# Where the residual rows, a quarter of a weight and the last splits of a one-core hybrid layer are placed

## The chip, the cores and the metric

The kernel runs on one core of a Trainium2 chip. A core has five engines that run side by side, each in its own order: TensorE (PE in the profile; its weight loads are PEld), VectorE (DVE), ScalarE (ACT), GpSimd (POOL) and SyncE (SP), which here issues most DMAs. Sixteen DMA engines move data between the device memory and the on-chip memory. Matmuls write to PSUM, everything else that is kept on the chip lies in SBUF.

The metric is the device time of one execution in microseconds (us), as the median of several. Inputs are laid out by the host before the launch, so that every weight load is one contiguous transfer of 1 MB.

## The reference

One decoder layer on 256 positions of width 2048. The parts that matter here are at its end: the state-space branch with its GLU, the merge of three branches, the output projection, the norm and the residual.

```python
h = rms_norm(x, pre_g)
proj = h @ w_in
a_u, a_v, a_g, b_x, b_g, x_q, x_g, gate_logits = jnp.split(proj, splits, axis=-1)
y_a = spatial_gating(a_u, a_v, sg_ln_g, sg_ln_b, sg_w, sg_b) * jax.nn.silu(a_g)
y_b = s5_branch(b_x, a_re, a_im, log_dt, b_re, b_im, c_re, c_im, d, glu_w, glu_b) * jax.nn.silu(b_g)
y_x = memory_cross_attention(x_q, rms_norm(mem, mem_g), xa_wk, xa_wv) * jax.nn.silu(x_g)
ys = jnp.stack([y_a, y_b, y_x], axis=2)
branch = jnp.einsum('bsnc,ncd->bsnd', ys, w_branch)
gates = jax.nn.sigmoid(gate_logits.reshape(bsz, seq, N_BRANCH, D_MODEL))
merged = jnp.sum(gates * branch, axis=2)
out = merged @ w_out
return x + rms_norm(out, post_g)
```

Inside `s5_branch` the last step is `y * sigmoid(y @ glu_w + glu_b)`. All is float32.

## The kernel before

**Arithmetic.** Each float32 operand of a product is split into a high part (`a.copy` on ACT, a cast to the type fp32r) and a low part (a subtraction on DVE), by `split_to`. A product is three matmuls: high by high, high by low, low by high. A weight of 1 MB is loaded by `load` into one of three `raw` buffers of 128 x 2048, and split in halves of 128 x 1024 into one of four `hl` buffers by `split`. So a `raw` buffer is free again when the subtractions of both its halves have run, and a cast into an `hl` buffer waits until PE has used the half that was four before it.

**Order.** PE's order is the program's. The order on the other engines, SP's DMAs among them, is fixed when the kernel is built: a planner takes, of what it thinks ready, the instruction of the earliest rank. The rank is the place in the program; `tc.high_priority(offset=AHEAD)`, which `split` uses, sets it 250 places ahead. Buffers of a pool are handed out in the planner's order as well. On the chip every engine then runs its own list strictly in order, so an instruction that waits holds up all behind it. `tc.keep_in_program_order` keeps marked instructions in the program's order.

**Stages at the end, with the start of each in the trace.** The gate product of the state-space branch runs up to 749 us. Then come:

- The GLU stage (749 to 770 us): four loads of `glu`; `ahead(0, ...)` splits half of the fourth quarter of the output weight into homes of its own (`room(8)`, `room(12)`: eight 128 x 512 tiles of the pool of h's splits, no longer needed), and `spread` loads the rows of `g_post` into `room(0)` and those of `x[0]` into `room(4)`, four DMAs of 256 KB each.
- The branch stage (770 to 812 us): for four column blocks c, two loads of `w_br`, products, gating and merging. `merge_t(c)`, run in the background by `pump`, transposes the merged block and makes the operands of the later products: the splits `mm`, and for a Strassen-like scheme on the first half of the depth and width of the output product the forms `S3` (from `r3`, kept with `r21` in the tile with tag `cb`) and, for c of 2 and 3, `S1`, `S2`, `S4`. The subtractions of `S1` and `S4` run on POOL.
- The output stage (from 812 us): `normal(0)`, `normal(1)`, `normal(2)`, product X, then the rows of `x[1]` by `spread` into four tiles of tag `s`, `normal(3)`, product Y, `narrow(0)`, product X by `S2` and a stored sum of weights (`wsum[1]`), `ahead(1, ...)` with the fourth quarter's other half into a tile of tag `cb` and one of tag `H2` (where `S2` was), `narrow(1)`, product Z by `S1` and `wsum[0]`, product Y by `S4` and the fourth quarter (`b22`), product Z by `S3` and `wsum[2]`, product X by `wsum[3]`.
- The last product (from 884.73 us): 256 columns, first the one half of the rows (tb 0), then the other. Its first half-load is split into `room(8)` and `room(12)`, its other three into `hl` buffers.
- The finish: squares, root, gain and residual, and the stores. `part` finds the tile and columns of `g_post` or `x` that a piece needs.

The matmuls of a weight half take 2.6 us in `normal` and 1.3 us in `product`; a 1 MB load takes some 4.8 us from issue to landing.

Of the kernel before, what the change touches and what calls it, by code (L numbers as in the profile page):

```python
# [9 lines left out]
F32 = mybir.dt.float32  # L10
F32R = mybir.dt.float32r
# [3 lines left out]
ALU = mybir.AluOpType  # L15
# [3 lines left out]
P = 128  # L19
D = 2048  # L20
# [13 lines left out]
AHEAD = 250  # L34
# [9 lines left out]
def trunk(ctx: ExitStack, tc: tile.TileContext, I, out):  # L44
    nc = tc.nc
    v, a, g, pe = nc.vector, nc.scalar, nc.gpsimd, nc.tensor
# [8 lines left out]
    s5p = ctx.enter_context(tc.tile_pool(name="s5p", bufs=2))  # L55
    s5c = ctx.enter_context(tc.tile_pool(name="s5c", bufs=1))
# [8 lines left out]
    def nm(s):  # L65
        n_[0] += 1
        return f"{s}_{n_[0]}"

    def slot(tag, shape, dt=F32):
        return big.tile(shape, dt, tag=tag, name=nm(tag))  # L70
# [5 lines left out]
    def load(src):  # L76
        t = rawp.tile([P, 2048], F32, tag="raw", name=nm("raw"))
        nc.sync.dma_start(out=t, in_=src)
        return t
# [8 lines left out]
            split_to(hi, lo, src)  # L88
        return hi, lo

    def split_to(hi, lo, src, eng=None):
        a.copy(out=hi, in_=src)  # L92
        (eng or v).tensor_tensor(out=lo, in0=src, in1=hi.bitcast(F32), op=ALU.subtract)  # L93

    def rsqrt(src, n):
        y = small([P, n])
# [136 lines left out]
    def tm_quarter(acc, raw, hl, kq, nk):  # L233
        for hf in range(2):
            wh, wl = split(raw[:, hf * 1024:(hf + 1) * 1024])
            for k in range(2):
                kk = kq * 4 + hf * 2 + k
                sl = slice(k * 512, (k + 1) * 512)
                for tb in range(2):
                    tm_mm(acc[tb], wh[:, sl], wl[:, sl], hl[kk], tb, kk == 0, kk == nk - 1)  # L240
            pump(rate["tm"])
# [23 lines left out]
    for pc in range(8):  # L265
# [6 lines left out]
        wh, wl = (z.rearrange("p (q n) -> p q n", q=2) for z in halves(CM_OFF))  # L272
# [680 lines left out]
    def room(i0):  # L953
        return [xp.tile([P, 512], F32R, tag=f"x{i0 + k}", name=nm("xr")) for k in range(4)]

    def ahead(kq, homes):
        raw = load(I["w_out"][1, 2 + kq])
        for k in range(4):
            t, i = homes[k // 2], k % 2
            split_to(t[i], t[2 + i], raw[:, k * 512:(k + 1) * 512])  # L960
            b22.append((t[i], t[2 + i]))

    post = {}

    def spread(key, src, homes):
        post[key] = [t.bitcast(F32) for t in homes]
        for k in range(4):
            tc.keep_in_program_order(nc.sync.dma_start(out=post[key][k], in_=src[:, k * 512:(k + 1) * 512]))

    sgB = [slot("H1", [P, D]), slot("H2", [P, D])]  # L970
    for c in range(4):
# [11 lines left out]
    for bp in range(4):  # L983
        ps = acc_tile()
        raw = load(I["glu"][bp])
        for b in range(2):
            wh, wl = split(raw[:, b * 1024:(b + 1) * 1024], CM_OFF)
            cm_half(ps[:, b], wh, wl, ygl, 0, 8)
        t = fold(ps, None)
        for i in range(2):  # L990
            a.activation(out=t[:, i, :], in_=t[:, i, :], func=AF.Sigmoid, bias=glu_b[:, 2 * bp + i:2 * bp + i + 1])
        b = slice(2 * bp, 2 * bp + 2)
        v.tensor_tensor(out=t, in0=t, in1=u[:, b, :], op=ALU.mult)
        v.tensor_tensor(out=t, in0=t, in1=sb[:, b, :], op=ALU.mult)
        for i in range(2):
            d = yB[2 * bp + i]
            split_to(d[:, 0], d[:, 1], t[:, i])
        if bp == 0:
            ahead(0, [room(8), room(12)])
        elif bp == 1:  # L1000
            spread("g", I["g_post"][0].broadcast_to([P, D]), room(0))
        elif bp == 2:
            spread(0, I["x"][0], room(4))

    yBs = [Plain(d, True) for d in yB]
    mm = {}
# [9 lines left out]
    S1, S2, S4 = [], [], []  # L1016

    def merge_t(c):
        yield from steps(3 if c >= 2 else 2)
        for hf in range(2):  # L1020
            tp = (yp if hf else miscp).tile([P, 2, T], F32, tag="y" if hf else "misc", name=nm("mt"))
            for i in range(2):
                db = c * 4 + hf * 2 + i
                for tb in range(2):
                    pe.transpose(tp[:, i, tb * P:(tb + 1) * P], mg[tb][:, db * P:(db + 1) * P], ident)
            yield None
            d = mm_tile(c)[:, 2 * hf:2 * hf + 2]
            split_to(d[:, :, 0], d[:, :, 1], tp)
            k = slice((c % 2) * 4 + 2 * hf, (c % 2) * 4 + 2 * hf + 2)
            lo_, up = tp[:, :, 0:P], tp[:, :, P:T]  # L1030
            if c < 2:
                a.copy(out=r21[:, k], in_=up)
                v.tensor_tensor(out=r3[:, k], in0=lo_, in1=r21[:, k], op=ALU.subtract)
                split_to(S3[:, k, 0], S3[:, k, 1], r3[:, k])
            else:
                if not S1:
                    S1.append(slot("H1", [P, 8, 2, P], F32R))
                    S2.append(slot("H2", [P, 8, 2, P], F32R))
                    S4.extend(s5p.tile([P, 2, 2, P], F32R, tag=f"P{i // 2 + 1}", name=nm("S4")) for i in range(4))
                t = wk.tile([P, 3, 2, P], F32, tag="w0", name=nm("sa"), padded_shape=[P, 4, 2, P])  # L1040
                tt(t[:, 0], r21[:, k], up, ALU.subtract)
                stt(t[:, 1], r3[:, k], -1.0, up, ALU.mult, ALU.subtract)
                tt(t[:, 2], lo_, t[:, 1], ALU.add)
                split_to(S1[0][:, k, 0], S1[0][:, k, 1], t[:, 0], g)
                split_to(S2[0][:, k, 0], S2[0][:, k, 1], t[:, 1])
                f = S4[k.start // 2]
                split_to(f[:, :, 0], f[:, :, 1], t[:, 2], g)
            if hf == 0:
                yield None

    def product(ps, form, src):
        for kk in range(8):
            if src is b22:
                wh, wl = src[kk]
            else:
                if kk % 4 == 0:
                    raw = load(src[kk // 4])
                if kk % 2 == 0:
                    hi, lo = split(raw[:, kk % 4 * 512:kk % 4 * 512 + 1024])
                sl = slice(kk % 2 * 512, (kk % 2 + 1) * 512)  # L1060
                wh, wl = hi[:, sl], lo[:, sl]
            f = form[kk]
            pe.matmul(ps, lhsT=f(0), rhs=two(wh), start=kk == 0, stop=False)  # L1063
            pe.matmul(ps, lhsT=f(0), rhs=two(wl), start=False, stop=False)  # L1064
            pe.matmul(ps, lhsT=f(1), rhs=two(wh), start=False, stop=kk == 7)  # L1065
            if kk % 4 == 3:
                pump(0.0)

    for c in range(4):
        Bp = acc_tile()  # L1070
        for kq in range(2):
            tm_quarter([Bp[:, 0], Bp[:, 1]], load(I["w_br"][1, c, kq]), yBs, kq, 8)
        for tb in range(2):
            d = sgB[tb][:, csl(c)]
            v.tensor_tensor(out=d, in0=Bp[:, tb], in1=d, op=ALU.mult)
            v.tensor_tensor(out=mg[tb][:, csl(c)], in0=mg[tb][:, csl(c)], in1=d, op=ALU.add)
        bg[2].append(merge_t(c))
# [9 lines left out]
        a.activation(out=t, in_=ps, func=AF.Square, scale=D ** -0.5, accum_out=ssq[:, tb, n:n + 1])  # L1087

    def part(key, lo_, hi_):
        return post[key][lo_ // 512][:, lo_ % 512:(hi_ - 1) % 512 + 1]  # L1090

    def gated(dst, ps, lo_, hi_):
        v.tensor_tensor(out=dst, in0=ps, in1=part("g", lo_, hi_), op=ALU.mult)
# [8 lines left out]
    def cut(t):  # L1102
        return [t[:, i] for i in range(4)]
# [28 lines left out]
    normal(1)  # L1132
    normal(2)
    product(X, a11, w_o[0, 0:2])
    spread(1, I["x"][1], [s5p.tile([P, 512], F32R, tag="s", name=nm("xs"), bufs=4) for _ in range(4)])
    sn = snap_tile()
    s1, c11 = sn[:, 0], sn[:, 1]
    a.copy(out=s1, in_=X)
# [2 lines left out]
    sq_out(1, N[:, 1], 2, csl(2))  # L1141
    gated(og[0][:, csl(2)], N[:, 0], 1024, 1536)
    gated(N[:, 1], N[:, 1], 1024, 1536)
    product(Y, a12, w_o[0, 2:4])
    tt(c11, s1, Y, ALU.add)
    sq_out(0, c11, 0, csl(0))
# [3 lines left out]
    sn = snap_tile()  # L1150
    s2, s5 = sn[:, 0], sn[:, 1]
    tt(s2, X, s1, ALU.add)
    ahead(1, [cut(s5c.tile([P, 4, 512], F32R, tag="cb", name="bq")), cut(slot("H2", [P, 4, 512], F32R))])
    narrow(1)
    sq_out(0, c3[0][:, 0:T], 3, slice(1536, 1792))
    sq_out(1, c3[1][:, 0:T], 3, slice(1536, 1792))
# [33 lines left out]
    for kh in range(2):  # L1190
        raw = load(I["w_out3"][1, kh])
        for hf in range(2):
            src = raw[:, hf * 1024:(hf + 1) * 1024]
            if kh == 0 and hf == 0:
                for i, t in enumerate((room(8), room(12))):
                    wh, wl = t[0], t[1]
                    split_to(wh, wl, src[:, i * 512:(i + 1) * 512])
                    wks += [(wh[:, k * T:(k + 1) * T], wl[:, k * T:(k + 1) * T]) for k in range(2)]
            else:
                wh, wl = split(src)  # L1200
                wks += [(wh[:, k * T:(k + 1) * T], wl[:, k * T:(k + 1) * T]) for k in range(4)]
# [13 lines left out]
    for tb in range(2):  # L1215
# [4 lines left out]
        c = slice(tb, tb + 1)  # L1220
# [118 lines left out]
```

## Time and profile before

| | before |
|---|---|
| median of 3 runs | 911.99 us (911.44 to 912.46) |
| profiled execution, its own time | 911.15 us |
| its span in the profile | 909.3 us |
| PE busy | 894.4 us (98%) |
| DVE busy | 787.4 us (87%) |
| ACT busy | 591.3 us (65%) |
| POOL busy | 78.6 us (9%) |
| DMA, mean over the span | 240 GB/s |
| PE's last matmul starts | 901.30 us |

Busy time is the time in which an engine has an instruction running. For PE it says little: matmuls overlap, and a PE that is slowed or waits for a fraction of a step still counts as busy. More can be read from the starts of its matmuls: two that follow without a wait start 0.22 us apart at 512 columns and 0.11 us apart at 256. In the timelines below, the first column is the start in us from the start of the span, the second the duration (of all, where xN instructions are merged into one row), then engine, line, operation, what is written and read, shapes; in brackets stands how long the engine was idle before, and what ended that. In the rows of windows, each engine has its busy time and its count in the order PE, PEld, DVE, ACT, POOL; then follow the granted TensorE clock, the DMA engines' busy share and GB/s. In the rows of waits stand the total in us, the number of waits and the longest.

### The profile page before, as it was taken

How to read it: one execution, taken by the hardware profiler on the slowest of the kernel's cores; microseconds unless marked ns; L12 is line 12 of the kernel's file. 1: busy time of each engine (PE TensorE's matmuls, PEld its weight loads, DVE VectorE, ACT ScalarE, POOL GpSimd, SP SyncE). 2: the span in 40 equal slices, each digit the busy share in tenths (PEclk: the TensorE clock that was granted, in tenths of full speed). 3: DMA queues.
4: the chain of work that ended last, by engine and by line, in shares of the span. 5: the costliest groups of instructions: out<-in, count | busy, mean ns of one | idle time of the engine just before them, and what ended most of it. 6: DMA issues, size and time to landing. Idle time of an engine off the chain costs nothing.

```text
span 909.3 us, 13209 instructions
## 1 busy us (share of the span) xinstructions
PE 894.4 (98%) x4872; PEld 794.2 (87%) x4872; DVE 787.4 (87%) x1236; ACT 591.3 (65%) x1018; POOL 78.6 (9%) x112
## 2 busy tenths in 40 slices
PE   9999999999999999999999999999999999999995
PEld 7999998899888888889999888888988888898975
DVE  6899877977887999899888799999997967889884
ACT  7585755876667676684645666867676566557671
POOL 1000000100011111211100112110010000003000
PEclk9999999999999999999999999999999999999998
DMA  9877766764568777999865768695655577557862
GB/s 337 336 283 276 252 232 240 261 197 139 187 213 239 220 290 198 373 292 292 265 219 181 249 235 241 226 263 210 236 199 189 198 255 288 187 188 265 309 254 93
DMA packets 37727, 218.37 MB, mean 240 GB/s; under 512 B 4896, under 2 KB 7456, under 8 KB 15392
## 3 DMA queue, kind: packets, MB, share of 16 engines
q1 hardware_dynamic: 30304, 192.11, 58.1%
q0 software_dynamic: 6496, 22.94, 11.5%
q10 hardware_dynamic: 864, 2.49, 0.7%
q8 instruction: 38, 0.62, 0.3%
q14 instruction: 25, 0.20, 0.1%
HBM read 213.46 MB, written 18.87 MB: 255 GB/s over the span
## 4 chain that ended last, share of the span: by engine, by line
PE 93%; DVE 2%; DMA 2%; ACT 1%; issue 1%; SPq 0%; DVEq 0%; ACTq 0%
PE acc L177 21%; PE acc L193 18%; PE acc L195 17%; PE acc L194 17%; PE acc L182 11%; DVE hl L93 1%; DMA raw<-glu 1%; PE y L646 1%; PE bu L584 1%; PE bx L177 1%; PE acc L1065 1%; PE acc L1063 1%; DMA st<-start 1%; PE acc L1064 1%; DMA raw<-wsum 1%; PE oacc L1123 1%
## 5 line engine op out<-in xcount | busy, mean ns | idle before, releaser
L93 DVE TENSOR_TENSOR hl<-raw,hl 128x1024 fp32r<-128x1024 f32 x327 | 398.0, 1224 | 82.7 <-ACT hl L92 81.5
L92 ACT CAST hl<-raw 128x1024 fp32r<-128x1024 f32 x327 | 338.8, 1045 | 185.4 <-PE acc L195 83.6
L177 PE MATMUL acc<-x,hl 128*128 128x512 f32 x736 | 218.5, 383 | 0.8 <-ACT hl L92 0.4
L193 PE MATMUL acc<-hl,x 128*128 128x512 f32 x448 | 170.7, 381 | 0.0
L194 PE MATMUL acc<-hl,x 128*128 128x512 f32 x448 | 169.8, 379 | 0.0
L195 PE MATMUL acc<-hl,x 128*128 128x512 f32 x448 | 169.8, 379 | 0.0
L182 PEld LDWEIGHTS acc<-x,hl 128*128 128x128 f32 x736 | 136.7, 189 | 18.8
L182 PE MATMUL acc<-x,hl 128*128 128x256 f32 x736 | 138.7, 274 | 0.0
L177 PEld LDWEIGHTS acc<-x,hl 128*128 128x128 f32 x736 | 113.6, 193 | 2.9 <-ACT hl L92 1.8
L193 PEld LDWEIGHTS acc<-hl,x 128*128 128x128 f32 x448 | 84.7, 189 | 13.6 <-issue 2.5
L195 PEld LDWEIGHTS acc<-hl,x 128*128 128x128 f32 x448 | 84.7, 189 | 12.0
L194 PEld LDWEIGHTS acc<-hl,x 128*128 128x128 f32 x448 | 84.8, 189 | 11.2
L555 POOL DMA_DIRECT2D B<-sb x30 | 26.9, 897 | 386.5 <-ACT B L550 358.6
L177 PE MATMUL acc<-H,hl 128*128 128x512 f32 x192 | 57.5, 381 | 0.4 <-DVE f L246 0.4
L193 PE MATMUL acc<-hl,H 128*128 128x512 f32 x144 | 54.9, 382 | 0.0
L194 PE MATMUL acc<-hl,H 128*128 128x512 f32 x144 | 54.6, 379 | 0.0
L195 PE MATMUL acc<-hl,H 128*128 128x512 f32 x144 | 54.6, 379 | 0.0
L390 DVE TENSOR_TENSOR p<-bu,E 128x512 f32<-128x512 f32 x64 | 41.7, 683 | 1.3 <-PE bu L584 1.0
L622 DVE TENSOR_TENSOR_SCAN p<-s5r,p 128x256 f32<-128x256 f32 x64 | 41.2, 679 | 0.6
L182 PEld LDWEIGHTS acc<-H,hl 128*128 128x128 f32 x192 | 36.1, 189 | 5.6 <-DVE hl L93 0.6
L182 PE MATMUL acc<-H,hl 128*128 128x256 f32 x192 | 37.0, 275 | 0.0
L538 POOL DMA_DIRECT2D sb<-s5b x32 | 19.0, 596 | 183.1 <-DMA B<-sb 135.3
(348 smaller groups left out, 1351.1 us busy)
## 6 DMA issues: line engine op xcount, KB each, us to landing
raw<-w_gate SPq DMA_DIRECT2D x48, 1024.0 KB, 4.8
raw<-w_br SPq DMA_DIRECT2D x24, 1024.0 KB, 5.0
raw<-w_out SPq DMA_DIRECT2D x14, 1024.0 KB, 4.8
raw<-w_xq SPq DMA_DIRECT2D x8, 1024.0 KB, 4.8
raw<-wk SPq DMA_DIRECT2D x8, 1024.0 KB, 4.7
raw<-wv SPq DMA_DIRECT2D x8, 1024.0 KB, 4.9
raw<-w_xg SPq DMA_DIRECT2D x8, 1024.0 KB, 5.1
wsum<-w_out POOLq DMA_DIRECT2D x16, 512.0 KB, 8.0
```

What stands on the lines that cost most here:

```text
L92: a.copy(out=hi, in_=src)
L93: (eng or v).tensor_tensor(out=lo, in0=src, in1=hi.bitcast(F32), op=ALU.subtract)
L177: pe.matmul(ps, lhsT=wh, rhs=hl.moving_both(), start=k == 0, stop=False)
L182: pe.matmul(h, lhsT=wl, rhs=hl.moving(0), start=False, stop=k == nk - 1)
L193: pe.matmul(ps, lhsT=hl.stationary(0, tb), rhs=two(wh), start=first, stop=False)
L194: pe.matmul(ps, lhsT=hl.stationary(0, tb), rhs=two(wl), start=False, stop=False)
L195: pe.matmul(ps, lhsT=hl.stationary(1, tb), rhs=two(wh), start=False, stop=last)
L390: v.tensor_tensor(out=o, in0=i0, in1=i1, op=op)
L538: g.dma_start(out=rw, in_=I["s5b"][q])
L555: g.dma_start(out=B4[64:P].bitcast(F32), in_=rw[64:P], accum_op=ALU.add)
L584: pe.matmul(bu[:, ri, :], lhsT=B4[:, ri, :], rhs=two(U4), start=True, stop=True)
L622: v.tensor_tensor_scan(out=p2[:, ri], data0=rb, data1=p1[:, ri], initial=0.0, op0=ALU.mult, op1=ALU.add)
```

## The change

It moves no arithmetic to another form; the same products are computed.

- `spread` takes pieces with their column bounds, and `part` looks a piece up by them. All three row loads now stand in the branch stage, one after each of its first three column blocks: `x[1]` after the first, into tiles that the state-space stage left (`left_by_s5`: two of tag `E`, one of tag `uhl`, five DMAs), `x[0]` after the second into `room(4)`, `g_post` after the third into `room(0)`.
- The tiles of tag `s` are thereby free for `ahead(1, ...)`: the second half of the fourth quarter goes to them and to `cb`, no longer to `H2`, and it stands right behind `normal(3)`, ahead of product Y, where it stood behind product X by `S2`.
- The subtractions of `S1` and `S4` go to DVE, as all others.
- The splits of the last product's first half-load get the same rank ahead (`AHEAD`) as `split` gives.

```diff
--- before.py
+++ after.py
@@ -88,9 +88,9 @@
             split_to(hi, lo, src)
         return hi, lo
 
-    def split_to(hi, lo, src, eng=None):
+    def split_to(hi, lo, src):
         a.copy(out=hi, in_=src)
-        (eng or v).tensor_tensor(out=lo, in0=src, in1=hi.bitcast(F32), op=ALU.subtract)
+        v.tensor_tensor(out=lo, in0=src, in1=hi.bitcast(F32), op=ALU.subtract)
 
     def rsqrt(src, n):
         y = small([P, n])
@@ -963,9 +963,20 @@
     post = {}
 
     def spread(key, src, homes):
-        post[key] = [t.bitcast(F32) for t in homes]
-        for k in range(4):
-            tc.keep_in_program_order(nc.sync.dma_start(out=post[key][k], in_=src[:, k * 512:(k + 1) * 512]))
+        post[key] = []
+        for lo_, hi_, t in homes:
+            t = t.bitcast(F32)
+            tc.keep_in_program_order(nc.sync.dma_start(out=t, in_=src[:, lo_:hi_]))
+            post[key].append((lo_, hi_, t))
+
+    def cols(tiles):
+        return [(k * 512, (k + 1) * 512, t) for k, t in enumerate(tiles)]
+
+    def left_by_s5():
+        e = [s5p.tile([P, 768], F32R, tag="E", name=nm("xe")) for _ in range(2)]
+        w = s5p.tile([P, 512], F32R, tag="uhl", name="xu", bufs=1)
+        return [(0, 256, e[0][:, 0:256]), (1024, 1536, e[0][:, 256:768]), (256, 512, e[1][:, 0:256]),
+                (1536, 2048, e[1][:, 256:768]), (512, 1024, w)]
 
     sgB = [slot("H1", [P, D]), slot("H2", [P, D])]
     for c in range(4):
@@ -997,10 +1008,6 @@
             split_to(d[:, 0], d[:, 1], t[:, i])
         if bp == 0:
             ahead(0, [room(8), room(12)])
-        elif bp == 1:
-            spread("g", I["g_post"][0].broadcast_to([P, D]), room(0))
-        elif bp == 2:
-            spread(0, I["x"][0], room(4))
 
     yBs = [Plain(d, True) for d in yB]
     mm = {}
@@ -1041,10 +1048,10 @@
                 tt(t[:, 0], r21[:, k], up, ALU.subtract)
                 stt(t[:, 1], r3[:, k], -1.0, up, ALU.mult, ALU.subtract)
                 tt(t[:, 2], lo_, t[:, 1], ALU.add)
-                split_to(S1[0][:, k, 0], S1[0][:, k, 1], t[:, 0], g)
+                split_to(S1[0][:, k, 0], S1[0][:, k, 1], t[:, 0])
                 split_to(S2[0][:, k, 0], S2[0][:, k, 1], t[:, 1])
                 f = S4[k.start // 2]
-                split_to(f[:, :, 0], f[:, :, 1], t[:, 2], g)
+                split_to(f[:, :, 0], f[:, :, 1], t[:, 2])
             if hf == 0:
                 yield None
 
@@ -1070,6 +1077,9 @@
         Bp = acc_tile()
         for kq in range(2):
             tm_quarter([Bp[:, 0], Bp[:, 1]], load(I["w_br"][1, c, kq]), yBs, kq, 8)
+        if c < 3:
+            spread(*((1, I["x"][1], left_by_s5()), (0, I["x"][0], cols(room(4))),
+                     ("g", I["g_post"][0].broadcast_to([P, D]), cols(room(0))))[c])
         for tb in range(2):
             d = sgB[tb][:, csl(c)]
             v.tensor_tensor(out=d, in0=Bp[:, tb], in1=d, op=ALU.mult)
@@ -1087,7 +1097,7 @@
         a.activation(out=t, in_=ps, func=AF.Square, scale=D ** -0.5, accum_out=ssq[:, tb, n:n + 1])
 
     def part(key, lo_, hi_):
-        return post[key][lo_ // 512][:, lo_ % 512:(hi_ - 1) % 512 + 1]
+        return next(t[:, lo_ - b:hi_ - b] for b, e, t in post[key] if b <= lo_ and hi_ <= e)
 
     def gated(dst, ps, lo_, hi_):
         v.tensor_tensor(out=dst, in0=ps, in1=part("g", lo_, hi_), op=ALU.mult)
@@ -1132,7 +1142,6 @@
     normal(1)
     normal(2)
     product(X, a11, w_o[0, 0:2])
-    spread(1, I["x"][1], [s5p.tile([P, 512], F32R, tag="s", name=nm("xs"), bufs=4) for _ in range(4)])
     sn = snap_tile()
     s1, c11 = sn[:, 0], sn[:, 1]
     a.copy(out=s1, in_=X)
@@ -1141,6 +1150,8 @@
     sq_out(1, N[:, 1], 2, csl(2))
     gated(og[0][:, csl(2)], N[:, 0], 1024, 1536)
     gated(N[:, 1], N[:, 1], 1024, 1536)
+    ahead(1, [[s5p.tile([P, 512], F32R, tag="s", name=nm("bs"), bufs=4) for _ in range(4)],
+              cut(s5c.tile([P, 4, 512], F32R, tag="cb", name="bq"))])
     product(Y, a12, w_o[0, 2:4])
     tt(c11, s1, Y, ALU.add)
     sq_out(0, c11, 0, csl(0))
@@ -1150,7 +1161,6 @@
     sn = snap_tile()
     s2, s5 = sn[:, 0], sn[:, 1]
     tt(s2, X, s1, ALU.add)
-    ahead(1, [cut(s5c.tile([P, 4, 512], F32R, tag="cb", name="bq")), cut(slot("H2", [P, 4, 512], F32R))])
     narrow(1)
     sq_out(0, c3[0][:, 0:T], 3, slice(1536, 1792))
     sq_out(1, c3[1][:, 0:T], 3, slice(1536, 1792))
@@ -1194,7 +1204,8 @@
             if kh == 0 and hf == 0:
                 for i, t in enumerate((room(8), room(12))):
                     wh, wl = t[0], t[1]
-                    split_to(wh, wl, src[:, i * 512:(i + 1) * 512])
+                    with tc.high_priority(offset=AHEAD):
+                        split_to(wh, wl, src[:, i * 512:(i + 1) * 512])
                     wks += [(wh[:, k * T:(k + 1) * T], wl[:, k * T:(k + 1) * T]) for k in range(2)]
             else:
                 wh, wl = split(src)
```

## The prediction

> **What bounds the kernel now.** I read the page first (span, busy shares, chain), then the waits of PE, then the timelines of the places where PE waited.
>
> ```profile
> PE 93%; DVE 2%; DMA 2%; ACT 1%; issue 1%; SPq 0%; DVEq 0%; ACTq 0%
> PE oacc L194 <- DVE xr L93: 3.8, 2, 3.2
> PE Z L1064 <- DVE hl L93: 0.8, 1, 0.8
> PE acc L177 <- DVE f L246: 0.4, 1, 0.4
> ```
>
> The chain is 93% PE: an edit gains only where PE stands still or is slowed, or behind its last matmul. The last three rows are all the waits of PE after 740 us: the last product (3.8 us, twice), the product into Z, the GLU product. The change touches what feeds each of them.
>
> ```profile
> 884.73 0.27 PE L193 MATMUL oacc<-xr,H 128*128 128x256 f32 x1
> 885.60 0.38 PE L194 MATMUL oacc<-xr,H 128*128 128x256 f32 x1 [0.60 <-DVE xr L93]
> ...
> 886.26 0.28 PE L193 MATMUL oacc<-xr,H 128*128 128x256 f32 x1
> 889.74 0.38 PE L194 MATMUL oacc<-xr,H 128*128 128x256 f32 x1 [3.21 <-DVE xr L93]
> ...
> 890.46 0.42 PE L193 MATMUL oacc<-hl,H 128*128 128x256 f32 x1
> ...
> 893.66 0.31 PE L193 MATMUL oacc<-hl,U 128*128 128x256 f32 x1
> ...
> 901.18 0.28 PE L194 MATMUL oacc<-hl,X 128*128 128x256 f32 x1
> 901.30 0.28 PE L195 MATMUL oacc<-hl,X 128*128 128x256 f32 x1
> 890.00:894.00 4.00, 4.00 (x23) 4.00 (x23) 0.00 (x0) 0.00 (x1) 0.00 (x0) 0.57 0.02 4
> ```
>
> The last product (first column: start) starts a matmul every 0.11 us (901.18, 901.30). Its second matmul waits for the low half of the first split, its next low half for the second. Then 15 steps from 890.46 to 893.66 take 3.20 us, 0.213 each; the last row, a window of 4 us, has a granted clock of 0.57 there (third figure from the end). So two waits cost three things: 885.60 − 884.84 = 0.76; 889.74 − 886.37 = 3.37; 3.20 − 15 × 0.111 = 1.53. Together 5.66.
>
> **The change, part by part.** *Rank of the last product's splits.*
>
> ```profile
> 879.46 0.61 ACT L92 CAST xr<-raw 128x512 fp32r<-128x512 f32 x1
> 880.92 0.62 ACT L92 CAST xr<-raw 128x512 fp32r<-128x512 f32 x1
> 884.86 0.68 DVE L93 TENSOR_TENSOR xr<-raw,xr 128x512 fp32r<-128x512 f32 x1
> 886.06 2.35 DVE L93 TENSOR_TENSOR hl<-raw,hl 128x1024 fp32r<-128x1024 f32 x2
> 889.00 0.68 DVE L93 TENSOR_TENSOR xr<-raw,xr 128x512 fp32r<-128x512 f32 x1
> ```
>
> The high halves (ACT) are done at 881.54; the low ones (DVE) run at 884.86 and 889.00, the second behind a pair of splits that PE needs later. Nothing is added: two subtractions of 0.68 and two casts of 0.6 move up, and no DMA. With the rank of the other splits both should run by about 884, before PE asks at 884.84 and 886.37: −5.66. Next late is the pair at 886.06 (its load's two halves), which PE wants at 887.5 and 888.8 (24 and 36 steps of 0.111 after 884.73, and one for the low half). The pair now ends at 888.4; one subtraction more ahead of it makes 888.4 + 0.6 = 889.0, against 888.8. I keep 0.3 for that (bounds 0 and 0.9).
>
> *Residual and gain rows, 3 MB.*
>
> ```profile
> 750.12 8.78 DMA raw<-glu
> 764.43 0.38 PE L182 MATMUL acc<-H,hl 128*128 128x256 f32 x2
> 765.19 0.67 PE L177 MATMUL acc<-H,hl 128*128 128x512 f32 x2 [0.38 <-DVE f L246]
> 750.00:760.00 10.00, 10.00 (x63) 9.17 (x62) 4.37 (x5) 4.98 (x8) 0.00 (x0) 1.00 0.98 362
> 766.00:812.00 46.00, 46.00 (x229) 41.56 (x228) 39.45 (x55) 26.66 (x42) 0.00 (x0) 1.00 0.56 201
> 817.00 2.25 SPq L968 DMA_DIRECT2D xs<-x  x4
> ```
>
> Before, 2 MB of rows share the GLU stage with its weights: DMA is 98% busy at 362 GB/s (last two figures), a GLU load takes 8.78 us, and the chain runs from it to a PE wait. Without the rows that load comes some 3 us sooner, so the matmul due at 764.65 (0.22 after 764.43) isn't held to 765.19: −0.54 (bounds −0.54 and 0). The rows go to the branch stage, 766 to 812, at 201 GB/s: 3 MB more in 46 us make 270. Thirteen DMAs on SP take some 0.56 us each to issue (2.25 for four), in three groups between loads of w_br.
>
> ```profile
> 763.80 0.33 SPq L78 DMA_DIRECT2D raw<-w_br  x1
> 773.55 1.05 ACT L92 CAST hl<-raw 128x1024 fp32r<-128x1024 f32 x1
> ```
>
> The load that the first group precedes is issued at 763.80, lands some 4.7 us later (the time of such a load in the stage after, quoted below) and is first cast at 773.55 (four split buffers pace the casts): 5 us to spare, against 2.8 of issuing or some 3 of sharing. I cost it at nothing; without that cover it would be up to 3 us a group. The new homes (E, uhl) were last used by the state-space stage, so no wait on them.
>
> *Two subtractions of each later transpose from POOL to DVE.*
>
> ```profile
> 829.88 1.78 DVE L93 TENSOR_TENSOR hl<-raw,hl 128x1024 fp32r<-128x1024 f32 x1
> 840.27 0.41 DVE L93 TENSOR_TENSOR H<-sa,H 128x256 fp32r<-128x256 f32 x1
> 831.00:842.00 11.00, 11.00 (x55) 9.66 (x54) 10.81 (x13) 8.53 (x12) 3.24 (x3) 1.00 0.70 252
> ```
>
> Two in each of four transposed halves: eight at 0.41 (840.27, POOL idle) add 3.3 us to DVE. But a split that runs beside POOL takes 1.78 where its like take 1.2 (886.06, two in 2.35): some 0.55 more. DVE has six such stretched rows beside POOL in its timeline from 822 to 835, so about 3.2 come back. Net nothing, between −3.2 and +3.3 of DVE time, in a stretch where DVE is busy 10.81 of 11 us; PE runs up to four split halves behind DVE and doesn't see it.
>
> *The fourth quarter's second half, sooner.* Its 1 MB load now stands between normal(3)'s and product Y's.
>
> ```profile
> 828.27 0.33 SPq L78 DMA_DIRECT2D raw<-w_out  x1
> raw<-w_out SPq DMA_DIRECT2D x1, 1024.0 KB, 4.7
> 833.70 0.33 SPq L78 DMA_DIRECT2D raw<-w_out  x1
> 837.33 0.41 DVE L393 SCALAR_TENSOR_TENSOR sa<-raws,mt 128x256 f32<-128x256 f32 x1
> 846.73 0.50 PE L1123 MATMUL oacc<-hl,H 128*128 128x256 f32 x3
> 849.66 0.69 DVE L1093 TENSOR_TENSOR acc<-acc,xr 128x512 f32<-128x512 f32 x1
> 852.94 1.29 DVE L93 TENSOR_TENSOR bq<-raw,bq 128x512 fp32r<-128x512 f32 x2
> 857.48 1.15 ACT L92 CAST H<-raw 128x512 fp32r<-128x512 f32 x2 [0.52 <-PE acc L1065]
> 858.42 5.83 DMA raw<-wsum
> 865.10 0.38 PE L1065 MATMUL Z<-hl,H 128*128 128x512 f32 x1
> 866.71 0.48 PE L1064 MATMUL Z<-hl,H 128*128 128x512 f32 x1 [0.78 <-DVE hl L93]
> ```
>
> Gain: before, half of its homes was H2, which product X reads; the casts into it waited for PE until 857.48, the load's buffer was held till then, and the loads of the sums (858.42) came late. Z lost 866.71 − (865.10 + 2 × 0.22) = 1.17. This goes: −1.17 (bounds −1.17 and 0).
>
> Price: three load buffers. The issue times 828.27 and 833.70 are when buffers fall free, paced by PE; they now serve the moved load and product Y's first. Y's first load lands at 833.70 + 4.7 = 838.4; its two casts (1.0 each) and subtractions (1.2 each) free its buffer at about 842.0. The moved load holds its own at least as long: half of its new homes is `cb`, whose old content (r3, r21) the transposes' arithmetic reads until about 837.7, and its four subtractions (0.64 each) queue on a full DVE behind the splits. So narrow(0)'s load is issued at 842.0, lands at 846.7, is cast by 847.8 and subtracted by 849.0. PE asks for that low half at 846.73 + 0.22 = 846.95: a wait of **2.1 us** that wasn't there. Queued behind it are all of PE's matmuls. If the moved load's buffer frees 2 us sooner, the wait is nothing; if narrow(0) must wait for that very buffer and it frees at 843, 3.0. I take 2.1, the sum from the nearest rows. Behind it the loads run some 4 us ahead.
>
> **Sum.** Against the profiled execution's own time (911.15, span 909.3 and 1.85 around it): −5.66 + 0.3 − 0.54 − 1.17 + 2.1 = −4.97, so 906.2. The median of the runs shown, 911.99, lies 0.84 higher; with that, **907.0**. What lies behind PE's last matmul (901.58 to 909.3) stays.
>
> **Rivals.** A. *No new wait*: the moved load's splits fit into DVE's gaps by 840. For it: Y's own splits now come later and leave a gap around 838. Against: DVE's 10.81 of 11 us. 907.0 − 2.1 = 904.9.
>
> B. *The new wait also halves the clock.* It grows to 3 us or more, and PE comes back as it did after 3.21 us: 1.5 more. 907.0 + 0.9 + 1.5 = 909.4. Against: after the 0.78 us wait at 866 no row shows a lower clock. [...]
>
> C. *The rank changes nothing*: DVE's order is fixed when the kernel is built, and the second low half could still stand behind the pair. Then 911.99 − 0.54 − 1.17 + 2.1 = 912.4. Against: the rank is that of splits which do run ahead of gatings.
>
> D, *slower*: narrow(0)'s load is tied to the moved load's buffer, and that buffer's last subtractions stand behind the gatings of N, which ran up to 850.3 before. Issued then, landing at 855.0, subtracted by 857.3: a wait of 10.4, and 1.5 at half clock. 907.0 − 2.1 + 11.9 = 916.8. It outweighs the gains of 7.1 once the buffer frees later than about 845.5 (5.6 of wait and 1.5 of clock). Against: a second buffer frees at 842.
>
> **How the numbers follow.** A measurement of this kernel can tell about 0.2% (1.8 us) from no change. Forecast (906.0 to 908.3) 0.5; A 0.22; B 0.1; C 0.08; D 0.05; 0.05 for what I don't see. Faster (below 910.2): forecast, A and B and a little of the rest, 0.85. Same: C and a little, 0.09. Slower: D and a little, 0.06. The range reaches from A with its bounds (904.3) over the forecast to B (909.8).
>
> **What would show it.** In the last product: steps of 0.11 from the first matmul, granted clock 1.00 after 885, both xr subtractions ahead of the last pair. No wait at Z and at L177. If the price is right, a PE wait of 1 to 3 us at the start of narrow(0) (L1123), with narrow(0)'s load issued at about 842. If A holds, no such wait. I'm wrong if PE waits in the branch stage, if the xr subtractions still stand last, or if a wait behind ACT's casts appears that I haven't placed.

## The result and the profile after

| | before | after |
|---|---|---|
| median | 912.23 us (911.44 to 913.33, 6 runs) | 906.36 us (905.51 to 907.29, 6 runs) |
| profiled execution, its own time | 911.15 us | 905.51 us |
| its span | 909.3 us | 903.8 us |
| DVE busy | 787.4 us | 788.7 us |
| POOL busy | 78.6 us | 69.1 us |
| PE's last matmul starts | 901.30 us | 895.76 us |

The ratio is 0.9936 (95% interval 0.9923 to 0.9949): 0.64% faster, against a forecast of 907.0 us. The lines have moved: the product's matmuls now stand at L1070 to L1072, narrow's at L1133; the split's subtraction is still L93.

First the waits of PE after 740 us, in the changed kernel (total, number, longest):

```profile
PE oacc L1133 <- DVE hl L93: 0.8, 1, 0.8
PE acc L1071 <- DVE hl L93: 0.3, 1, 0.3
```

All three waits of before are gone, 5.0 us in all; two new ones came, 1.1 us. PE's timeline of the changed kernel shows the old places and the new ones:

```profile
764.60 0.39 PE L182 MATMUL acc<-H,hl 128*128 128x256 f32 x2
764.82 0.60 PE L177 MATMUL acc<-H,hl 128*128 128x512 f32 x2
...
843.53 0.38 PE L1070 MATMUL acc<-hl,X 128*128 128x512 f32 x1
844.26 0.48 PE L1071 MATMUL acc<-hl,X 128*128 128x512 f32 x1 [0.35 <-DVE hl L93]
...
846.52 0.38 PE L1072 MATMUL acc<-hl,X 128*128 128x512 f32 x1
846.99 0.49 PE L1133 MATMUL oacc<-hl,H 128*128 128x256 f32 x2
848.24 5.40 PE L1133 MATMUL oacc<-hl,H 128*128 128x256 f32 x46 [0.77 <-DVE hl L93]
...
865.11 0.38 PE L1072 MATMUL Z<-hl,H 128*128 128x512 f32 x1
865.32 0.38 PE L1070 MATMUL Z<-hl,H 128*128 128x512 f32 x1
...
884.75 0.27 PE L193 MATMUL oacc<-xr,H 128*128 128x256 f32 x1
884.85 0.28 PE L194 MATMUL oacc<-xr,H 128*128 128x256 f32 x1
...
887.42 0.27 PE L193 MATMUL oacc<-hl,U 128*128 128x256 f32 x1
887.84 0.38 PE L194 MATMUL oacc<-hl,U 128*128 128x256 f32 x1
```

Starts tell more than the waits in brackets. At the GLU product (764.60 to 764.82) and at Z (865.11 to 865.32) a step is the plain 0.22 us. At product Y the first matmul that needs a low half of its second load starts 0.73 us after the one before it instead of 0.22: 0.51 lost. Narrow's first two start at 846.99, which is 0.25 later than 846.52 + 0.22, and the third, due at 846.99 + 2 × 0.11 = 847.21, starts at 848.24: 1.03 more, so 1.28 lost there, and 1.79 at both places. The last product loses 0.31, at 887.84 (0.42 after 887.42 instead of 0.11).

The windows over the last product, of the changed kernel (busy time and count of PE, PEld, DVE, ACT, POOL, then granted clock, DMA share, GB/s):

```profile
885.00:890.00 5.00, 4.86 (x44) 4.67 (x43) 4.90 (x7) 2.84 (x5) 0.00 (x0) 1.00 0.00 0
890.00:894.00 4.00, 4.00 (x39) 4.00 (x38) 2.46 (x11) 2.42 (x7) 0.00 (x0) 1.00 0.00 0
```

In the four microseconds from 890 the clock was 0.57 with 23 matmuls before; it is 1.00 with 39 now. The splits of that product, in DVE's timeline of the changed kernel:

```profile
879.67 0.69 DVE L93 TENSOR_TENSOR xr<-raw,xr 128x512 fp32r<-128x512 f32 x1
...
881.63 0.68 DVE L93 TENSOR_TENSOR xr<-raw,xr 128x512 fp32r<-128x512 f32 x1
...
886.57 2.35 DVE L93 TENSOR_TENSOR hl<-raw,hl 128x1024 fp32r<-128x1024 f32 x2
```

The two subtractions of the first half-load end at 882.31 (before: 885.54 and 889.68), and the pair that PE wants afterwards ends at 888.92.

Where the moved load went is seen on SP, DVE and ACT, in the timeline of the changed kernel:

```profile
827.12 0.33 SPq L78 DMA_DIRECT2D raw<-w_out  x1
...
832.74 0.33 SPq L78 DMA_DIRECT2D raw<-w_out  x1
...
835.94 0.33 SPq L78 DMA_DIRECT2D raw<-w_out  x1
...
838.57 2.36 DVE L93 TENSOR_TENSOR hl<-raw,hl 128x1024 fp32r<-128x1024 f32 x2
...
840.96 0.33 SPq L78 DMA_DIRECT2D raw<-w_out  x1
...
845.89 1.99 ACT L92 CAST hl<-raw 128x1024 fp32r<-128x1024 f32 x2 [0.83 <-DMA raw<-w_out]
```

The loads are, in order, the moved one, product Y's two and narrow(0)'s. The DVE row holds the subtractions of Y's first load: they end at 838.57 + 2.36 = 840.93, and narrow(0)'s load is issued 0.03 us later, into the buffer that they free. ACT then stands idle for its landing before it casts: the wait comes from the load, as the last bracket says.

Last, SP's row of the first group of row loads (`x[1]`), the stage that took the other rows, and the DVE stretches of the transposes, as windows, all of the changed kernel:

```profile
757.25 2.19 SPq L969 DMA_DIRECT2D xe<-x  x4
750.00:760.00 10.00, 10.00 (x62) 9.20 (x61) 6.30 (x7) 6.17 (x10) 0.00 (x0) 1.00 0.86 309
766.00:812.00 46.00, 46.00 (x230) 41.80 (x229) 38.96 (x54) 26.61 (x42) 0.00 (x0) 1.00 0.68 237
815.00:831.00 16.00, 16.00 (x81) 14.05 (x80) 15.72 (x29) 9.77 (x18) 0.00 (x0) 1.00 0.54 193
831.00:842.00 11.00, 11.00 (x52) 9.66 (x51) 10.68 (x17) 8.63 (x15) 0.00 (x0) 1.00 0.57 201
```

The GLU stage's DMA fell from 0.98 to 0.86, the branch stage's rose from 0.56 to 0.68 (237 GB/s), and PE waits nowhere in it. The `x[1]` rows stand behind the first column block in the program, but SP issues them at 757.25, still in the GLU stage, if behind its last weight load (750.29). Before, both groups of rows went out between the GLU loads, at 740.71 and 746.87. The last GLU load now lands after 4.7 us, where it took 8.78.

### The profile page after: what moved, and what is told of

The parts are those of the page before. It is cut to its first block, busy times and chain, and to the rows that moved or that the text cites. A ratio compares the mean times of both kernels' runs of the same rounds, so it can differ in the third digit from the quotient of the medians.

```text
span 903.8 us, 13201 instructions
## 1 busy us (share of the span) xinstructions
PE 892.3 (99%) x4872; PEld 793.7 (88%) x4872; DVE 788.7 (87%) x1244; ACT 591.4 (65%) x1018; POOL 69.1 (8%) x104
## 4 chain that ended last, share of the span: by engine, by line
PE 85%; DVE 7%; DMA 4%; ACT 2%; issue 2%; SPq 0%; DVEq 0%; ACTq 0%
PE acc L193 18%; PE acc L195 17%; PE acc L194 17%; PE acc L177 17%; PE acc L182 9%; DVE hl L93 3%; DMA raw<-w_out 2%; DMA M<-mem 2%; ACT hl L92 1%; PE oacc L1133 1%; PE y L646 1%; PE bu L584 1%; DVE H L172 1%; DMA st<-start 1%; PE po L761 1%
## 5 line engine op out<-in xcount | busy, mean ns | idle before, releaser
L93 DVE TENSOR_TENSOR hl<-raw,hl 128x1024 fp32r<-128x1024 f32 x327 | 396.9, 1221 | 80.3 <-ACT hl L92 78.1
```

The source lines that it names most:

```text
L93: v.tensor_tensor(out=lo, in0=src, in1=hi.bitcast(F32), op=ALU.subtract)
```

## The experiments

The theory was that the rank of the last product's splits carries the gain, that the rows free the GLU wait for nothing, and that the quarter's move cures Z and pays for it at Y and narrow(0). The rivals put the gain, or the loss, elsewhere. Each ratio is against the kernel before, timed beside it.

**e1: the rank alone.** The kernel before, with one line:

```diff
-                    split_to(wh, wl, src[:, i * 512:(i + 1) * 512])
+                    with tc.high_priority(offset=AHEAD):
+                        split_to(wh, wl, src[:, i * 512:(i + 1) * 512])
```

> The kernel before with one edit: the rank of the last product's first splits. Theory: both waits of the last product and the stretch at half clock go, 5.66 us, less 0.3 for the last pair of splits: 5.4 us faster than before, ratio 0.994; the wait of 1.2 us in the product into Z stays. Rival 1: the earlier loads of the whole change are needed for it, and without them ACT and DVE aren't ready: at most 3 us, ratio 0.997. Rival 2: the slow steps at 890 don't come from the waits: they stay somewhere in the last product, 3.9 us, ratio 0.996.

Measured: 905.49 us (5 runs; before 911.89), ratio 0.9926 (0.9913 to 0.9938). PE's waits in e1, after 740 us:

```profile
PE Z L1064 <- DVE hl L93: 0.8, 1, 0.8
PE acc L177 <- DVE f L246: 0.4, 1, 0.4
```

The last product's wait is gone, the other two stand as before. Its 96 matmuls take 10.60 us from the first start to the last (885.09 to 895.69); they took 16.57 before and 11.01 in the changed kernel. One line gives as much as the whole change: the other parts together come to nothing that can be measured. The medians lie 6.40 us apart, and the last product became 16.57 − 10.60 = 5.97 us shorter. The profiled execution of the kernel before is one of several kinds: in its 43 timed executions beside the experiments the mean granted clock lies between 0.992 and 0.997, and the 19 with 0.994 or less took 912.9 us in the mean, the other 24 took 911.3. The profiled one has 0.995.

**e2: the rows alone.** The changed kernel with the quarter at its old place and in its old homes, subtractions on POOL, and the old rank (the reverse of these hunks of the diff).

> The change's row loads alone (x[1], x[0], g_post in the branch stage, x[1] in E and uhl); the fourth quarter's second half at its old place and in its old homes, S1 and S4 on POOL, the old rank. Theory: the wait at the end of the GLU stage goes, 0.5 us, and nothing comes in the branch stage: ratio 0.9994; the waits at Z (1.2 us) and in the last product stay. Rival: the 3 MB delay w_br, PE waits in the branch stage: up to 3 us slower, ratio above 1.001.

Measured: 911.22 us (11 runs; before 911.89), ratio 0.9992 (0.9983 to 1.0001). PE's waits in e2:

```profile
PE oacc L194 <- DVE xr L93: 3.8, 2, 3.2
PE Z L1071 <- DVE hl L93: 0.6, 1, 0.6
PE oacc L1133 <- DVE hl L93: 0.5, 1, 0.5
```

The GLU wait is gone, and no wait came in the branch stage, so the rows do there what was said. The time can't tell 0.54 us from nothing. A wait of 0.5 in narrow(1) is new; e3 has one of 0.3 at the same place, e6 has none, and I don't explain it.

**e3: the old place with the new homes, and e6: the old place and the old homes.** In e3 the call of `ahead(1, ...)` goes back behind product X, but keeps its new homes; in e6 the homes go back too. All else is as changed.

```diff
-    ahead(1, [[s5p.tile([P, 512], F32R, tag="s", name=nm("bs"), bufs=4) for _ in range(4)],
-              cut(s5c.tile([P, 4, 512], F32R, tag="cb", name="bq"))])
     product(Y, a12, w_o[0, 2:4])
...
     tt(s2, X, s1, ALU.add)
+    ahead(1, ...)
```

> The changed kernel with the fourth quarter's second half loaded and split at its old place (behind product X by S2), but in the new homes (s, cb). Theory: the two new waits (0.5 us in product Y, 1.3 us in narrow(0)) come from the place, and the wait at Z came from the home H2: so neither is there, 1.8 us faster than the changed kernel, ratio to before 0.992 (904.6 us). Rival: it is the place that cured Z: its 1.2 us come back, 905.8 us, ratio 0.993.

> The changed kernel with the move of the fourth quarter's second half undone (old place, old homes cb and H2); rows in the branch stage, DVE subtractions and rank stay. Theory: the move is worth about nothing in sum: no wait in product Y and at the start of narrow(0), but the 1.2 us at Z (and narrow(1)) are back: within 0.7 us of the changed kernel, faster rather than slower. Rival: the move is a gain in itself of 1.2 us or more: slower than the changed kernel by that.

Measured: e3 904.45 us (4 runs), ratio 0.9916 (0.9903 to 0.993); e6 904.55 us (5 runs), ratio 0.992 (0.9905 to 0.9935). Beside e6 the changed kernel itself was timed again as **e5**:

> The changed kernel as it is, beside the three that follow on the same chip. Theory (from the run with the rank alone, 0.9926): the rank is worth all of the gain, and the rest of the change comes to nothing (0.5 at GLU and 1.2 at Z gained, 1.8 in product Y and narrow(0) lost): ratio 0.993. Rival: the rest costs: 0.9945.

It gave 905.15 us (6 runs; before 911.41), ratio 0.9931 (0.9915 to 0.9946). So the move is worth nothing, or slightly less than nothing; the intervals overlap. The waits of PE in e3 show why the time came out and the reason didn't:

```profile
PE Z L1071 <- DVE hl L93: 0.8, 1, 0.8
PE oacc L1133 <- DVE hl L93: 0.3, 1, 0.3
```

Z still waits (its step is 1.26 us in e3 and in e6, as before), though nothing goes into H2 any more. The home alone doesn't cure it. The second of the loads of the sums is the one that Z waits for; here are its issue, its time from issue to landing and ACT's cast in e3, then its issue and its time to landing in the changed kernel:

```profile
855.86 0.33 SPq L78 DMA_DIRECT2D raw<-wsum  x1
raw<-wsum SPq DMA_DIRECT2D x1, 1024.0 KB, 8.1
864.02 1.99 ACT L92 CAST hl<-raw 128x1024 fp32r<-128x1024 f32 x2 [2.60 <-DMA raw<-wsum]
```

```profile
856.08 0.32 SPq L78 DMA_DIRECT2D raw<-wsum  x1
raw<-wsum SPq DMA_DIRECT2D x1, 1024.0 KB, 5.2
```

In e3 the load isn't issued later than in the changed kernel, it lands later: after 8.1 us instead of 5.2, and ACT is idle for 2.60 us until then. In e6, with the old homes, it goes out at 857.61 and lands after 5.9 us. So home H2 did hold a buffer back, as the forecast had it (the quarter's is free at 859.38 in e6, at 855.83 in e3), but with that cured the load lands no sooner (864.0 in e3, 863.5 in e6). What cures Z is the place. That bunching is the reason is argued only: three loads of the sums go out within 3.5 us in e3 (854.65, 855.86, 858.13), and within 6.4 us in the changed kernel (852.95, 856.08, 859.38); no run moves these loads alone.

**e4: the subtractions back on POOL.** The changed kernel with `split_to(..., g)` for S1 and S4.

> The changed kernel with the subtractions of S1 and S4 on POOL, as before. Theory: DVE's time is the same within 0.5 us (eight subtractions of 0.41 less, six stretched by 0.55 more), and PE's waits in product Y and narrow(0) change by less than 0.5 us: ratio to before 0.993 to 0.994, as the changed kernel. Rival: DVE is what frees the moved load's buffer late, so with POOL's help narrow(0) waits at least 1 us less (ratio 0.9925), or with the stretching 1 us more (0.995).

Measured: 905.44 us (5 runs), ratio 0.9927 (0.9915 to 0.994), no different in time from the changed kernel. Windows of e4:

```profile
815.00:831.00 16.00, 16.00 (x81) 14.03 (x80) 15.52 (x24) 10.46 (x18) 7.10 (x6) 1.00 0.55 197
831.00:842.00 11.00, 11.00 (x52) 9.64 (x51) 10.84 (x14) 8.04 (x14) 3.57 (x3) 1.00 0.60 200
```

Eight subtractions fewer, and DVE is busy 15.52 + 10.84 = 26.36 us, against 15.72 + 10.68 = 26.40: what DVE is spared, it loses beside POOL. Most of that isn't in the 128x1024 splits (1.28 us in the mean from 815 to 842, against 1.22) but in the four 128x256 subtractions that stay on DVE beside POOL's (0.82 against 0.42). PE's recorded waits at Y and in narrow were 2.2 us, against 1.1: the expectation that they change by less than 0.5 fell, though the time doesn't show it.

**e7: the quarter without a load buffer.** The price of the move was said to be a load buffer. `og[1]` isn't written before the end of the stage, so the 1 MB can go there and be split from there:

```diff
-    def ahead(kq, homes):
-        raw = load(I["w_out"][1, 2 + kq])
+    def ahead(kq, homes, raw=None):
+        raw = load(I["w_out"][1, 2 + kq]) if raw is None else raw
...
     product(Y, a12, w_o[0, 2:4])
+    nc.sync.dma_start(out=og[1], in_=I["w_out"][1, 3])
...
     narrow(0)
+    ahead(1, [[... "s" tiles ...], cut(... "cb" ...)], og[1])
```

> The changed kernel, but the fourth quarter's second half is loaded into the tile of og[1] (tag M1: free from the last transposes to the last product) and not into one of the three load buffers; it is issued behind product Y's first load and split from there into the same homes. Theory: both waits come from load buffers: with all three left to the other loads, no wait over 0.3 us is left between the GLU stage and the last product: 1.8 us faster than the changed kernel, ratio 0.991. Rival: the wait in product Y and narrow(0) is one of DMA rate or of DVE's time: it stays, and the time is that of the changed kernel, 0.993.

Measured: 902.69 us (6 runs, 902.51 to 905.02; before 911.41), ratio 0.9905 (0.9888 to 0.9921); 2.46 us below the changed kernel on the same chip. After 740 us no wait of PE is left in its trace. SP's timeline of e7:

```profile
830.23 0.33 SPq L1154 DMA_DIRECT2D M<-w_out  x1
832.19 3.53 SPq L78 DMA_DIRECT2D raw<-w_out  x2
```

The first is the quarter, into `og[1]`; behind it come product Y's second load and narrow(0)'s, the latter now issued at 835.39 (832.19 + 3.53 − 0.33) instead of 840.96. With the buffer given back, the wait is gone. The quarter's splits also stand later in e7, behind narrow(0)'s; the two weren't tried apart. The waits at Y and narrow(0) account for 1.8 of the 2.46 us, and the last product for another 0.2 (its 96 matmuls take 10.78); the rest isn't placed.

**e8 to e12: what one wait of PE does to the clock.** The forecast had 2.1 us of new wait cost only itself, and rival B had 3 us as the least that halves the clock. In the changed kernel a subtraction is repeated into the low half that the last product needs at its 26th matmul:

```diff
                 wh, wl = split(src)
+                if kh == 1 and hf == 0:
+                    with tc.high_priority(offset=AHEAD):
+                        v.tensor_tensor(out=wl, in0=src, in1=wh.bitcast(F32), op=ALU.subtract)
```

That is e8, with all 1024 columns; e9 repeats 128 of them, e10 512.

> The changed kernel with one more subtraction (the same one again) into the low half that the last product needs at its 26th matmul. It makes one wait of about 2.4 us there, in the place of 0.3, and nothing before it. Theory: a wait of 2.4 us costs itself alone, the matmuls after it start 0.11 us apart: 2.1 us slower than the changed kernel. Rival: it halves the clock, as the two waits of the kernel before did: some 15 steps of 0.21 us, 3.7 us slower.

> As the run with one more subtraction, but of 128 columns only: one wait of about 1.4 us at the last product's 26th matmul. The run before showed that one wait of 2.2 us is enough for the half clock. Theory: the half clock needs a wait between 0.8 us (seen without it) and 2.2 us (seen with it); at 1.4 us I expect none: steps of 0.11 us after the wait, 1.1 us later than the changed kernel. Rival: any wait over 1 us brings it: 16 steps of 0.21 us, 1.6 us more.

> The same with 512 columns: one wait of about 1.8 us. [...]

One execution of each: 911.45 us (before 911.41), 907.29 and 906.05 us (before 911.0). PE's timeline of e8:

```profile
889.43 0.28 PE L193 MATMUL oacc<-hl,U 128*128 128x256 f32 x1
891.88 0.38 PE L194 MATMUL oacc<-hl,U 128*128 128x256 f32 x1 [2.17 <-DVE hl L1215]
...
892.98 0.40 PE L194 MATMUL oacc<-hl,U 128*128 128x256 f32 x1
...
896.37 0.30 PE L195 MATMUL oacc<-xr,H 128*128 128x256 f32 x1
```

The steps are 0.11 us until 892.98; then 16 steps take 3.39 us, 0.21 each, until 896.37. The windows of e8 have the clock to it; the first two are cut at 893.00, where it falls, and 3.41 us before and behind:

```profile
889.59:893.00 3.41, 1.24 (x12) 1.12 (x11) 3.38 (x4) 0.54 (x1) 0.00 (x0) 1.00 0.00 0
893.00:896.41 3.41, 3.41 (x19) 3.41 (x18) 0.65 (x4) 1.83 (x5) 0.00 (x0) 0.50 0.00 0
906.00:907.00 1.00, 0.00 (x0) 0.00 (x0) 0.00 (x0) 0.00 (x0) 0.00 (x0) 0.83 0.98 364
```

My expectation fell: one wait of 2.17 us halved the clock, and it cost 3.66 us (14.67 for the last product's 96 matmuls, against 11.01): 2.34 of wait instead of the 0.31, and 1.6 of slow steps. The rest of its 6 us over the changed kernel lies elsewhere: this execution had reached the last product 2.0 us later. In e9 (a wait of 1.24) and e10 (1.64) the clock stayed at 1.00; that e10's wait, put at 1.8 us, would bring the drop too was my estimate, and it fell. It looked like a threshold somewhere between 1.64 and 2.17 us. So the kernels of e8 and e10 ran again, timed:

> The kernel of e8 again, timed, to see whether the half clock behind its wait comes each time. The wait at the last product's 26th matmul is 2.0 to 2.3 us in every execution. If a wait of that length always halves the clock, the profile shows 0.75 and 0.50 again for some 3.4 us, and all times lie together, about 2.0 + 1.6 = 3.6 us above the changed kernel (some 909 us). If it depends on where the wait falls in a window that runs on its own, the times fall into two groups some 1.6 us apart (907.2 and 908.8), and this profile may show steps of 0.11 and a clock of 1.00 behind a wait of the same length.

> The kernel of e10 again, timed. Its wait is 1.5 to 1.8 us. If the threshold lies above that, every time lies some 1.3 us above the changed kernel (about 906.5 us), the profile shows a clock of 1.00, and e11 is slower by 0.6 + 1.6 = 2.2 us. If it is a matter of where the wait falls, some times here are 1.6 us higher too, and the median lies less than 2.2 us below that of e11.

Measured: e11 908.77 us (10 runs, 907.65 to 911.4; before 912.43), ratio 0.9966 (0.9952 to 0.9981); e12 908.32 us (7 runs, 906.91 to 909.04), ratio 0.9957 (0.9942 to 0.9972). PE's timeline of e11, and its windows, with one of e10 last:

```profile
890.44 0.38 PE L194 MATMUL oacc<-hl,U 128*128 128x256 f32 x1 [2.18 <-DVE hl L1215]
```

```profile
886.22:889.63 3.41, 2.04 (x19) 1.85 (x17) 3.38 (x5) 1.47 (x3) 0.00 (x0) 1.00 0.00 0
889.63:893.04 3.41, 2.60 (x23) 2.60 (x24) 2.55 (x6) 2.01 (x3) 0.00 (x0) 1.00 0.00 0
903.00:904.00 1.00, 0.00 (x0) 0.00 (x0) 0.00 (x0) 0.00 (x0) 0.00 (x0) 0.64 0.99 369
```

```profile
884.83:888.24 3.41, 1.77 (x16) 1.58 (x16) 3.41 (x5) 1.25 (x3) 0.00 (x0) 1.00 0.00 0
898.00:899.00 1.00, 0.00 (x0) 0.00 (x0) 1.00 (x2) 0.81 (x2) 0.51 (x1) 0.74 0.00 0
```

The same wait, 2.18 us, and this time a clock of 1.00 behind it: it isn't the length of the wait alone. The traces show what else. Where one holds several changes of the clock, they lie a whole number of times 3.41 us apart. In e8 it falls at 893.00, rises at 896.41 and falls again, behind the last matmul, at 906.66 (0.83 in the window from 906), which is 3 × 3.41 later. In the kernel before it falls at 890.32, rises 3.41 later and falls again after another 10.24, which is 3 × 3.41; its windows, the first of them the 3.41 us ahead of the first fall:

```profile
886.91:890.32 3.41, 0.58 (x5) 0.58 (x6) 3.02 (x7) 1.69 (x4) 0.00 (x0) 1.00 0.00 0
890.33:893.73 3.40, 3.40 (x19) 3.40 (x18) 0.00 (x0) 0.00 (x0) 0.00 (x0) 0.50 0.02 5
893.74:903.97 10.23, 7.83 (x70) 7.64 (x69) 5.44 (x16) 2.34 (x8) 0.22 (x1) 1.00 0.27 103
903.98:909.00 5.02, 0.00 (x0) 0.00 (x0) 1.25 (x2) 0.09 (x1) 1.17 (x2) 0.50 0.57 209
```

The traces' records of the clock give full speed for 884.05 us until its first fall in the kernel before and for 894.29 in the changed kernel: 259 and 262 times a third of 10.24. So the traces read as if each execution had a grid of 3.41 us of its own, and the fall behind the last matmul shows where it lies. In e11 that fall is at 903.28 (0.64 in the window from 903), and 4 × 3.41 before it, at 889.63, a grid point cuts the wait in two: PE is busy for 2.04 us of the one piece and 2.60 of the next. In e8 the whole wait lies in one piece, and PE is busy for 1.24 us of it. In e10 (fall at 898.48) the wait of 1.64 us lies in one piece too, and PE is busy for 1.77. So the clock was halved behind pieces with 0.58 (the kernel before) and 1.24 us (e8) of busy PE, and not behind pieces with 1.77 (e10) or 2.04 and 2.60 (e11).

How often that happened in e11 can be read from the mean granted clock of each execution. It is 0.998 or 0.999 in seven of the ten and 0.996 in three (909.1, 911.3 and 911.4 us). A half clock for 3.41 us takes 0.0019 off it, and the fall behind the last matmul, 2.7 (e8) to 5.5 us (e10) before the end in the traces, takes 0.0015 to 0.0031. By this estimate 0.996 has such a drop in it and 0.998 has none. All of e12's have 0.998 or 0.999. The medians of e11 and e12 lie only 0.45 us apart, since by the same estimate most of e11's executions have no drop. e12's own expectation of some 906.5 us fell, by 1.8 us; the kernel before was 1.0 us slower on that chip than beside e5, and the rest stays open.

## Why the prediction was right

**The rank: −5.66, with 0.3 kept.** Right. Two subtractions ended at 882.31, ahead of PE's 884.75; all three costs went (two waits and the half clock), and the pair behind them ended at 888.92, where 889.0 was forecast. The cost of 0.31 came at the pair's first half, at PE's 26th matmul; the forecast had weighed its second half (889.0 against 888.8), for which PE did not wait. The 96 matmuls became 16.57 − 11.01 = 5.56 us shorter. e1 shows this part alone; rival C, that the rank does nothing, is out.

**The rows: −0.54 and nothing.** Right. The GLU step is 0.22 again, in e2 as well, and PE doesn't wait in the branch stage. SP was ahead of what I assumed: the first group of rows was issued at 757, before the branch stage began, and the stage ran at 237 GB/s instead of 270.

**POOL to DVE: net nothing.** Right: 26.40 us of DVE against 26.36 in e4. The time that came back did so mostly on the 128x256 subtractions, not on the 128x1024 splits that the forecast named.

**Z: −1.17.** The size held, the reason failed. I had put the late loads of the sums down to home H2, which held a load buffer until PE was done with it. In e3 the homes are other ones and the load of a sum is issued sooner than in e6, but it lands no sooner, and Z waits the same 0.8 us. The place decides; why the load takes 8.1 us to land there, against 5.2, isn't shown.

**The new wait: +2.1.** The mechanism was right, the size 0.3 too large, and it came in two pieces: 0.51 at product Y's second load, which I had not placed, and 1.28 at narrow(0). Narrow(0)'s load waited for the buffer of Y's first load, as forecast, but that came free at 840.93, 1.1 us sooner than the 842.0 of the forecast. Y's second load took 5.9 us to land, and ACT stood idle for it for 1.06. In e7, where the quarter takes no load buffer, narrow(0)'s load is issued 5.6 us sooner and both waits are gone. Rival A (no new wait) is out, and so is D: narrow(0)'s load was issued 1.5 us before the moved load's buffer came free (841.18 + 1.28 = 842.46).

**Rival B** did not occur, but its condition was wrong. It asked for 3 us or more, and a wait of 2.17 us was enough in e8, where it lay in one piece of the grid. That 2.1 us costs only itself was my estimate: it held in e11 (2.18 us, clock 1.00) and not in e8. So 2.1 us in one wait could have cost 1.5 more in some executions. It came as two waits of at most 0.8 us in the records, and the clock stayed.

**Sum.** −5.56 − 0.54 − 1.17 + 1.79 = −5.48; the span fell by 909.3 − 903.8 = 5.5. That the sum fits so closely is partly luck: another execution of the changed kernel, e5's, has a span of 904.9. The median lies 0.85 above the profiled execution, where the forecast had added 0.84. The gain of the whole is that of one of its parts, since −0.54 − 1.17 and +1.79 cancel.

## What to carry to other kernels

Where an engine waits for an operand whose inputs were ready long before, look at the order on the engine that makes it: two subtractions of 0.68 us at the wrong rank cost 5.6 us, and one line gave them back. A load moved ahead in a ring of buffers takes its buffer from the loads behind it (narrow(0)'s went out at 840.96, against 835.39 in e7); a tile that is idle until later can hold it instead (e7). Before a cause is named for a late load, undo that cause alone: the home seemed to explain Z's wait, and with the home changed Z waited as long.

## What was not expected of the hardware

Behind one wait of PE of 2.17 us the granted clock was 0.50 for 3.41 us (e8, 893.00 to 896.41), starting 1.1 us after PE had resumed; behind an equal wait of 2.18 us it stayed at 1.00 (e11). Behind waits of 1.24 us (e9) and 1.64 us (e10, e12) it stayed at 1.00 as well. In these traces the clock changed at points 3.41 us, or a whole number of times that, apart, and what told the cases from each other is how long PE was busy in one such piece: behind 0.58 (the kernel before) and 1.24 us (e8) of 3.41 the clock was halved, behind 1.77 (e10) and more it was not. Whether one bound lies between 1.24 and 1.77 us of busy PE, and whether it is the same in other kernels, no run shows.
